# A decoder block at batch 1: another order for the opening, the background loads, the norm and the closing

## The chip, the cores and the metric

The kernel runs on one core of one Trainium2 chip, as a single launch. The metric is the device time of that core in microseconds (us): before the change 1770.57 us, the median of three runs (1770.28 to 1771.84). Smaller is better.

## The reference, cut to what matters

One layer of a decoder block over 256 tokens of width 2048, all in float32:

```python
mod = (silu(c) @ ada_w + ada_b)          # shift_m, scale_m, gate_m, shift_f, scale_f, gate_f
h = rmsnorm(x) * (1 + scale_m) + shift_m
p = h @ w_in                             # gla q,k,v,output gate,decay; mla q and kv latents, rope key; two gates
y_gla = (rmsnorm(gla_chunked(q, k, v, log_a)) * silu(p_g)) @ gla_wo     # 4 heads
y_mla = mla_attention(...) @ mla_wo                                     # 16 heads, rotary part
x = x + gate_m * ((sigmoid(p_ga) * y_gla + sigmoid(p_gb) * y_mla) @ w_out)
h = rmsnorm(x) * (1 + scale_f) + shift_f
x = x + gate_f * ((silu(h @ W_g) * (h @ W_u)) @ ffn_w_down)             # hidden width 5632
return rmsnorm(x)
```

## The kernel before

**Weights.** Each weight is read from DRAM once, in halves of two k-tiles of 128 rows by 512 columns (512 KB, `load_raw`, L100). ScalarE casts a half to a high part (L111), VectorE subtracts to get the low part (L112), and `form_a` (L164) or `form_b` multiplies both with the high and low part of the activations: three products per tile (L170 to L172), 12 matmuls of 512 columns a half in `form_a`. The raw tiles are a ring of six, with more of them where `more_raw` lends other memory; the high and low tiles are rings of three.

**The order.** The program is written engine by engine in one Python order; a planner with a model of the engines then decides, for each engine, which of its ready instructions is issued next, and the engines run that list in order. So an instruction may be issued far ahead of where it is written. `tc.keep_in_program_order(i)` puts `i` behind the instruction written before it on the same engine, without a wait for its end.

**Background work.** The modulation vectors come from `ada_w`, six blocks of 2048 columns. `ada_steps(m, c0)` (L270) is a generator that loads eight halves, one a yield, and leaves two VectorE dots for each (L282, L284); for m of 2, 3 and 4 it then reduces over the partitions on GpSimd (L294) and yields once more. `tick()` (L158) comes after each weight half: it issues the dots left, takes `pace[0]` more yields from the list `bg`, and moves two lanes of attention work on by a step. `background(1000)` (L871) takes all that is left.

**The stages.** The opening (L398 to L425) loads x, broadcasts silu(c) into `crow`, squares and transposes x, takes 1/rms by Newton steps (`rsqrt_mean`, L195), spreads it along the free axis (`rows_of`, L211), and forms the first two k-tiles of shift and scale by dots with `ada_t` (`ada_cols`, L247). `rope_angles` (L348) reduces the rotary angles on GpSimd, `rope_tables` (L382) turns them into sine and cosine. Four passes over `w_in` follow (r = 0 to 3), each with 16 jobs; `rope_tables` is called after the job of index 0 in the last pass. Then eight pairs of MLA heads with seven ticks each (`mla_pair`, L612; `pace` 0.2, L728), beside the GLA attention; the output gate O_G with 32 ticks (L781, 0.6), in whose first head the MLA heads still live are stepped to their end (L783 to L785); `mla_wo` with 32 ticks (0.8); `gla_wo` with 32 (0.65, L822); `w_out` with eight for each of four column groups (0.6, L855). In the last of these, i = 3, `background(1000)` runs first, and the last two halves are kept and multiplied token tile by token tile (L883). Then the norm: x1 is squared with a running sum (L890), 32 transposes fill x1T (L905), and 16 modulations (`modulate`, L318) give the input of the FFN. The FFN's halves follow, then `ffn_w_down`, whose last four k-tiles are held and multiplied at the end, block by block, with the closing behind each block: gate (L1008), add (L1009), square (L1011), for two of four blocks a multiply with the final gain on GpSimd (L1013), and after the fourth the sum, the Newton steps and the scalings (L1014 to L1023).

## Time and profile before

| | |
|---|---|
| median of three runs | 1770.57 us |
| the profiled execution | 1769.9 us |
| its span, first to last instruction | 1768.1 us |
| TensorE busy | 1694.1 us, 96% |
| VectorE busy | 1235.1 us, 70% |
| ScalarE busy | 832.2 us, 47% |
| GpSimd busy | 121.2 us, 7% |
| mean granted TensorE clock | 0.98 |
| DMA | 418.31 MB, mean 237 GB/s |

PE is TensorE, PEld its weight loads, which run beside it; DVE is VectorE, ACT ScalarE, POOL GpSimd, SP the engine that issues most of the DMA. DMA rates count all queues. The span is shorter than the execution by what lies ahead of the first instruction and behind the last. Busy times of different engines overlap, so they don't add up to the span; what counts is where the engine with the most work waits, and what ended that wait.

### The profile page before, as it was taken

What the parts mean: (1) busy time and instruction counts of PE and PEld (TensorE: products, weight loads), DVE (VectorE), ACT (ScalarE), POOL (GpSimd) and SP (SyncE); (2) the same over time, 40 slices, a digit from 0 to 9 for tenths busy, and PEclk for the clock granted to TensorE, in tenths of its full rate; (3) what the DMA queues carried; (4) which work ended last, traced back from release to release, by engine and by line L of the source; (5) the groups of instructions that cost most, each with busy time, mean ns of one, the idle gap of its engine ahead of it and who ended that gap; (6) DMA issues with size and microseconds to landing.
All of it is one profiled execution on the core that took longest, in us unless ns stands there. A gap on an engine that the chain in (4) does not pass through costs nothing.

```text
span 1768.1 us, 23022 instructions
## 1 busy us (share of the span) xinstructions
PE 1694.1 (96%) x8388; PEld 1427.0 (81%) x8388; DVE 1235.1 (70%) x1797; ACT 832.2 (47%) x1154; POOL 121.2 (7%) x139
## 2 busy tenths in 40 slices
PE   4999999999999999999996799999999999999997
PEld 2998899889998887788884588888888888788885
DVE  5999977587786477999887767667664444555556
ACT  4644434356666555444442254444444444444443
POOL 5000000000000111110011100000000000000001
PEclk7999999999999999999998899999999999999999
DMA  8999986655545487999997658788786666555552
GB/s 300 355 349 322 322 249 195 187 190 150 171 117 187 158 297 242 357 367 317 323 345 261 238 155 273 236 251 270 237 248 189 189 191 190 178 190 187 187 186 108
DMA packets 196074, 418.31 MB, mean 237 GB/s; under 512 B 13060, under 2 KB 23636, under 8 KB 195320
## 3 DMA queue, kind: packets, MB, share of 16 engines
q1 hardware_dynamic: 194136, 410.27, 71.0%
q0 software_dynamic: 1680, 6.51, 1.0%
q8 instruction: 66, 1.08, 0.2%
q14 instruction: 48, 0.39, 0.1%
q10 hardware_dynamic: 144, 0.07, 0.0%
HBM read 410.49 MB, written 6.30 MB: 236 GB/s over the span
## 4 chain that ended last, share of the span: by engine, by line
PE 90%; DVE 4%; POOL 2%; issue 2%; DMA 1%; ACT 1%; DVEq 0%; ACTq 0%; POOLq 0%
PE mm L171 20%; PE mm L172 20%; PE mm L170 20%; PE mm L180 3%; PE mm L181 3%; PE mm L182 3%; PE mm L959 2%; PE mm L960 2%; PE mm L961 2%; PE gx L685 2%; PE gx L960 1%; PE aux L960 1%; PE aux L959 1%; PE gx L959 1%; PE aux L961 1%
## 5 line engine op out<-in xcount | busy, mean ns | idle before, releaser
L112 DVE TENSOR_TENSOR lo<-raw,hi 128x1024 fp32r<-128x1024 f32 (+3 forms) x518 | 599.7, 1163 | 356.6 <-ACT hi L111 354.3
L111 ACT CAST hi<-raw 128x1024 fp32r<-128x1024 f32 (+3 forms) x518 | 506.5, 984 | 567.6 <-PE mm L172 400.1
L171 PE MATMUL mm<-lo,s 128*128 128x512 f32 (+1 forms) x1648 | 647.1, 393 | 2.4 <-DVE lo L112 2.2
L172 PE MATMUL mm<-hi,s 128*128 128x512 f32 (+1 forms) x1648 | 640.9, 390 | 0.0
L170 PE MATMUL mm<-hi,s 128*128 128x512 f32 (+1 forms) x1648 | 587.1, 392 | 22.8 <-ACT hi L111 21.6
L170 PEld LDWEIGHTS mm<-hi,s 128*128 128x128 f32 x1648 | 310.3, 189 | 88.7 <-ACT hi L111 24.3
L171 PEld LDWEIGHTS mm<-lo,s 128*128 128x128 f32 x1648 | 311.8, 189 | 67.5 <-DVE lo L112 6.0
L172 PEld LDWEIGHTS mm<-hi,s 128*128 128x128 f32 x1648 | 311.7, 189 | 61.6 <-issue 0.7
L284 DVE SCALAR_TENSOR_TENSOR ada<-raw,cact,ada 128x512 f32<-128x512 f32 x191 | 143.0, 749 | 15.4 <-DMA raw<-in_ada_w_dram 12.8
L111 ACT CAST hi<-s 128x1024 fp32r<-128x1024 f32 (+1 forms) x65 | 67.5, 1039 | 114.5 <-PE mm L172 66.6
L180 PE MATMUL mm<-s,hi 128*128 128x256 f32 x416 | 118.5, 287 | 0.0
L181 PE MATMUL mm<-s,hi 128*128 128x256 f32 x416 | 117.4, 284 | 0.0
L182 PE MATMUL mm<-s,lo 128*128 128x256 f32 x416 | 115.4, 285 | 0.0
L112 DVE TENSOR_TENSOR lo<-s,hi 128x1024 fp32r<-128x1024 f32 (+1 forms) x65 | 80.3, 1236 | 32.0 <-ACT hi L111 31.6
L180 PEld LDWEIGHTS mm<-s,hi 128*128 128x128 f32 x416 | 79.6, 191 | 0.8 <-issue 0.3
L181 PEld LDWEIGHTS mm<-s,hi 128*128 128x128 f32 x416 | 79.6, 191 | 0.4
L182 PEld LDWEIGHTS mm<-s,lo 128*128 128x128 f32 x416 | 78.3, 191 | 0.0
L960 PE MATMUL mm<-lo,w 128*128 128x512 f32 x160 | 63.6, 398 | 0.0
L294 POOL PARTITION_ALL_REDUCE ada<-ada x12 | 45.2, 3763 | 269.5 <-DVE ada L284 269.5
L961 PE MATMUL mm<-hi,w 128*128 128x512 f32 x160 | 62.6, 393 | 0.0
L959 PE MATMUL mm<-hi,w 128*128 128x512 f32 x160 | 50.9, 396 | 0.7 <-ACT w L968 0.7
L968 ACT CAST w<-s 128x256 fp32r<-128x256 f32 x44 | 17.7, 408 | 59.1 <-PE aux L960 59.1
(274 smaller groups left out, 1694.4 us busy)
## 6 DMA issues: line engine op xcount, KB each, us to landing
raw<-in_ffn_w_in_dram SPq DMA_DIRECT2D x176, 512.0 KB, 4.5
raw<-in_w_in_dram SPq DMA_DIRECT2D x124, 512.0 KB, 4.9
raw<-in_ada_w_dram SPq DMA_DIRECT2D x102, 512.0 KB, 4.8
raw<-in_ffn_w_down_dram SPq DMA_DIRECT2D x88, 512.0 KB, 4.4
raw<-in_ada_t_dram SPq DMA_DIRECT2D x44, 512.0 KB, 5.9
s<-in_ada_w_dram SPq DMA_DIRECT2D x26, 512.0 KB, 6.7
s<-in_w_in_dram SPq DMA_DIRECT2D x23, 512.0 KB, 4.4
raw<-in_mla_wo_dram SPq DMA_DIRECT2D x20, 512.0 KB, 5.6
```

The lines of the kernel that those rows point to most:

```text
L111: A.copy(out=hh_, in_=rr)
L112: V.tensor_tensor(out=ll_, in0=rr, in1=hh_.bitcast(F32), op=ALU.subtract)
L170: T.matmul(ps[t][:, :cols], lhsT=ah[:, k, ts], rhs=hi, start=st, stop=False)
L171: T.matmul(ps[t][:, :cols], lhsT=ah[:, k, ts], rhs=lo, start=False, stop=False)
L172: T.matmul(ps[t][:, :cols], lhsT=al[:, k, ts], rhs=hi, start=False, stop=en)
L180: T.matmul(o, lhsT=hi[:, pick], rhs=ah[:, k], start=st, stop=False, skip_group_check=True)
L181: T.matmul(o, lhsT=hi[:, pick], rhs=al[:, k], start=False, stop=False, skip_group_check=True)
L182: T.matmul(o, lhsT=lo[:, pick], rhs=ah[:, k], start=False, stop=en, skip_group_check=True)
L284: ins = V.scalar_tensor_tensor(out=acc, in0=raw[:, k - k0], scalar=c, in1=acc, op0=ALU.mult, op1=ALU.add)
L959: T.matmul(o, lhsT=ah[:, ts], rhs=hi[:, ns], start=first, stop=False)
L960: T.matmul(o, lhsT=ah[:, ts], rhs=lo[:, ns], start=False, stop=False)
L961: T.matmul(o, lhsT=al[:, ts], rhs=hi[:, ns], start=False, stop=last)
```

## The change

No product is added or left out; orders change.

- Opening: the copies of `crow` come first; x and the first eight loads of `ada_t` are issued in one fixed order (x's first half, four loads, x's second half, four loads), the dots in the same order on VectorE, six of them ahead of the Newton steps and two behind; the Newton steps and the scaled identity are pinned one behind the other. `ada_cols` is split into `ada_dots` and `ada_mod`. `rope_angles` is written later, and the instructions of `rope_tables` are pinned where they are written.
- Pace: 0.2 becomes 0.4 in the MLA stage, 0.65 becomes 0.8 in `gla_wo`, 0.6 becomes 0.75 in `w_out`.
- Heads: the stepping of the last MLA heads to their end leaves the first head of O_G; two slots for the GLA output are taken where they are first needed (`og_slots`), which steps the heads to their end if they still live.
- Norm: the transposes from k = 4 on are issued behind the last matmul of `w_out`; the casts of the second and third half split after the norm's modulations are issued behind the last Square.
- Closing: the first token tile's four scalings are one VectorE instruction each, issued behind the second tile's adds; the second tile's two multiplies with the gain move from GpSimd to VectorE.

`follow(a, b)` puts `a` behind `b` on their engine in the same way as the pin. Cut to its core:

```diff
         for rr, hh_, ll_ in ((raw, hv, lv),) if perm is None else perm(raw, hv, lv):
-            A.copy(out=hh_, in_=rr)
+            h = A.copy(out=hh_, in_=rr)
+            if fence:
+                follow(h, fence.pop(0))
             V.tensor_tensor(out=ll_, in0=rr, in1=hh_.bitcast(F32), op=ALU.subtract)
         return [(hv[:, k], lv[:, k]) for k in range(kk)]
+
+    fence = []
+
+    def follow(ins, prev):
+        if prev is not None:
+            tc.add_manual_dep(ins.ins, prev.ins.name, mybir.DependencyInfo(
+                mybir.DependencyClass.NoSync, mybir.DependencyReason.DATA), reason="order on one engine")
...
+        return mm
...
-    def rsqrt_mean(dst, ssq, n, w, eng=None):
+    def rsqrt_mean(dst, ssq, n, w, eng=None, pinned=False):
         v, l = sb(w, "rv"), sb(w, "rl")
+        pin = tc.keep_in_program_order if pinned else lambda i: i
+        pin(V.tensor_scalar(out=v, in0=ssq, scalar1=1.0 / n, scalar2=EPS, op0=ALU.mult, op1=ALU.add))
...
-    def rows_of(col, dst):
+    def rows_of(col, dst, pinned=False):
+        pin = tc.keep_in_program_order if pinned else lambda i: i
...
-    def ada_cols(k, now=False):
+    def ada_dots(k, now=False):
         for m in (1, 0):
...
                 raw = raw_tile()
-                nc.sync.dma_start(out=raw, in_=ada_t[m * D + k * P:m * D + (k + 1) * P, hf * 1024:(hf + 1) * 1024])
+                d = nc.sync.dma_start(out=raw, in_=ada_t[m * D + k * P:m * D + (k + 1) * P, hf * 1024:(hf + 1) * 1024])
...
                 if now:
-                    dot()
+                    tc.keep_in_program_order(d)
+                    tc.keep_in_program_order(dot())
                 else:
...
         flush()
+
+    def ada_mod(k):
         V.scalar_tensor_tensor(out=mod[:, 16 + k:17 + k], in0=mod[:, 16 + k:17 + k], scalar=1.0, in1=nmg[:, k:k + 1],
...
         modulate(k, xTk, rx, 0, hhk, hlk)
+
+    def ada_cols(k):
+        yield from ada_dots(k)
+        ada_mod(k)
...
         four = sb(512, "sc", 2)
-        V.scalar_tensor_tensor(out=ang2, in0=ang, scalar=-1.0, in1=ang, op0=ALU.mult, op1=ALU.max)
+        pin(V.scalar_tensor_tensor(out=ang2, in0=ang, scalar=-1.0, in1=ang, op0=ALU.mult, op1=ALU.max))
         V.tensor_scalar(out=ang2, in0=ang2, scalar1=-1.0, scalar2=float(np.float32(np.pi / 2)), op0=ALU.mult,
...
         for i, a in enumerate((ang, ang2)):
-            A.copy(out=four[:, i * S:(i + 1) * S].rearrange("p (t r f) -> p t r f", t=2, r=4),
-                   in_=a.rearrange("p (t f) -> p t f", t=2).unsqueeze(2).broadcast_to([P, 2, 4, 32]))
-            for t in range(2):
-                c = slice(i * S + t * P, i * S + (t + 1) * P)
-                T.transpose(out=ps[:, c], in_=four[:, c], identity=ident)
-        A.activation(out=sin_t, in_=ps[:, 0:S], func=AF.Sin, scale=sgn)
+            pin(A.copy(out=four[:, i * S:(i + 1) * S].rearrange("p (t r f) -> p t r f", t=2, r=4),
+                       in_=a.rearrange("p (t f) -> p t f", t=2).unsqueeze(2).broadcast_to([P, 2, 4, 32])))
+        for i in range(4):
+            c = slice(i * P, (i + 1) * P)
+            pin(T.transpose(out=ps[:, c], in_=four[:, c], identity=ident))
+        pin(A.activation(out=sin_t, in_=ps[:, 0:S], func=AF.Sin, scale=sgn))
         A.activation(out=cos_t, in_=ps[:, S:2 * S], func=AF.Sin)
...
     sx, rc2 = sb(2, "sx"), sb(2, "rx")
-    for t in range(2):
-        tc.keep_in_program_order(nc.sync.dma_start(out=xtok[:, t], in_=x[0, t * P:(t + 1) * P]))
-    ang, ang2 = rope_angles()
+    pin = tc.keep_in_program_order
     for b in range(4):
...
         T.matmul(ps, lhsT=ones, rhs=d, start=True, stop=True)
-        A.copy(out=crow[:, 512 * b:512 * (b + 1)], in_=ps)
+        pin(A.copy(out=crow[:, 512 * b:512 * (b + 1)], in_=ps))
+    more_raw((qk, 0, 4))
+    first = [ada_dots(k, True) for k in range(2)]
     for t in range(2):
-        A.activation(out=vt[:, 0:2048], in_=xtok[:, t], func=AF.Square, accum_out=sx[:, t:t + 1])
+        pin(nc.sync.dma_start(out=xtok[:, t], in_=x[0, t * P:(t + 1) * P]))
+        pin(A.activation(out=vt[:, 0:2048], in_=xtok[:, t], func=AF.Square, accum_out=sx[:, t:t + 1]))
+        for _ in range(4 - 2 * t):
+            next(first[t])
     for k in range(0, KT, 2):
         x_blocks(k)
-    rsqrt_mean(rc2, sx, D, 2)
-    rows_of(rc2, rx)
-    more_raw((qk, 0, 4))
+    rsqrt_mean(rc2, sx, D, 2, pinned=True)
+    rows_of(rc2, rx, pinned=True)
+    for _ in first[1]:
+        pass
+    for _ in first[0]:
+        pass
+    ang, ang2 = rope_angles()
     for k in range(2):
-        for _ in ada_cols(k, True):
-            pass
+        ada_mod(k)
     lat = slot(4)
...
         bg += [ada_steps(m, 512 * b) for m in (4, 3)]
-    pace[0] = 0.2
+    pace[0] = 0.4
     GLA.wait += [gla_att(h) for h in range(GH)]
...
     gtv = gt.rearrange("p (t d) -> p t d", t=2)
-    ogh, ogl = slot(6, F32R), slot(7, F32R)
-    oghk, oglk = k256(ogh), k256(ogl)
+    og = []
+
+    def og_slots():
+        if not og:
+            while ATT.busy():
+                ATT.step()
+            og[:] = [k256(slot(i, F32R)) for i in (6, 7)]
+        return og
...
         yield
+        oghk, oglk = og_slots()
         for k in range(0, 4, 2):
...
         ps = full(form_a, w_in, O_G + 512 * h, hhk, hlk, KT)
-        if h == 0:
-            while ATT.busy():
-                ATT.step()
+        assert h < 2 or not ATT.busy()
         if h == 0:
...
-    pace[0] = 0.65
+    pace[0] = 0.8
     mh, ml = slot(2, F32R), slot(1, F32R)
...
     for i in range(4):
-        for n, ps in enumerate(group(form_a, gla_wo, 512 * i, oghk, oglk, KT)):
+        for n, ps in enumerate(group(form_a, gla_wo, 512 * i, *og, KT)):
             tick()
...
     sq = sb(8, "sq")
-    pace[0] = 0.6
+    pace[0] = 0.75
...
             for k, w in kept:
-                form_a(ps, w, k256(mh), k256(ml), k, False, k == KT - 2, 512, (t,))
+                last = form_a(ps, w, k256(mh), k256(ml), k, False, k == KT - 2, 512, (t,))
             u = sb(512, "sc", 2)
...
             V.tensor_tensor(out=x1v[:, t, cs], in0=x1v[:, t, cs], in1=u, op=ALU.add)
-            A.activation(out=u, in_=x1v[:, t, cs], func=AF.Square, accum_out=sq[:, j:j + 1])
+            sqr = A.activation(out=u, in_=x1v[:, t, cs], func=AF.Square, accum_out=sq[:, j:j + 1])
             if j in (3, 5):
...
             for t in range(2):
-                T.transpose(out=ps[:, kk * S + t * P:kk * S + (t + 1) * P],
-                            in_=x1v[:, t, (k + kk) * P:(k + kk + 1) * P], identity=ident)
+                tp = T.transpose(out=ps[:, kk * S + t * P:kk * S + (t + 1) * P],
+                                 in_=x1v[:, t, (k + kk) * P:(k + kk + 1) * P], identity=ident)
+                if k >= 4:
+                    follow(tp, last)
         A.copy(out=x1T[:, k * S:(k + 2) * S], in_=ps)
...
         modulate(k, x1k, r2, 3, k256(fh), k256(fl))
+    fence[:] = [None, sqr, sqr]
     more_raw()
...
     otv = ot.rearrange("p (t d) -> p t d", t=2)
+    def finish(t, fr, behind):
+        for n, prev in zip((2, 0, 3, 1), behind):
+            ns = slice(n * 512, (n + 1) * 512)
+            if n < 2 and t:
+                A.activation(out=otv[:, t, ns], in_=x1v[:, t, ns], func=AF.Copy, scale=fr)
+            else:
+                follow(V.scalar_tensor_tensor(out=otv[:, t, ns], in0=x1v[:, t, ns], scalar=fr, in1=fg[:, ns],
+                                              op0=ALU.mult, op1=ALU.mult), prev)
+            nc.sync.dma_start(out=out[0, t * P:(t + 1) * P, ns], in_=otv[:, t, ns])
+
+    frs = []
     for t in range(2):
...
         fr = sb(1, "fr", 2)
+        adds = []
         for n in range(4):
...
             V.tensor_tensor(out=u, in0=acc[t][n], in1=gate_f[:, ns], op=ALU.mult)
-            V.tensor_tensor(out=d, in0=d, in1=u, op=ALU.add)
+            adds.append(V.tensor_tensor(out=d, in0=d, in1=u, op=ALU.add))
             junk = sb(512, "sc", 2)
             A.activation(out=junk, in_=d, func=AF.Square, accum_out=fs[:, n:n + 1])
-            if n < 2:
-                G.tensor_tensor(out=d, in0=d, in1=fg[:, ns], op=ALU.mult)
+            if n < 2 and t:
+                V.tensor_tensor(out=d, in0=d, in1=fg[:, ns], op=ALU.mult)
         V.tensor_reduce(out=f1, in_=fs, axis=AX.X, op=ALU.add)
         rsqrt_mean(fr, f1, D, 1)
-        for n in (2, 0, 3, 1):
-            ns = slice(n * 512, (n + 1) * 512)
-            if n < 2:
-                A.activation(out=otv[:, t, ns], in_=x1v[:, t, ns], func=AF.Copy, scale=fr)
-            else:
-                V.scalar_tensor_tensor(out=otv[:, t, ns], in0=x1v[:, t, ns], scalar=fr, in1=fg[:, ns],
-                                       op0=ALU.mult, op1=ALU.mult)
-            nc.sync.dma_start(out=out[0, t * P:(t + 1) * P, ns], in_=otv[:, t, ns])
+        frs.append(fr)
+    finish(0, frs[0], (adds[1], adds[2], adds[3], adds[3]))
+    finish(1, frs[1], (None,) * 4)
```

## Rows read from the trace of the kernel before

**Rows 1.** The page: engines' busy time; TensorE's slices; issues of one load.

```profile
PE 1694.1 (96%) x8388; PEld 1427.0 (81%) x8388; DVE 1235.1 (70%) x1797; ACT 832.2 (47%) x1154; POOL 121.2 (7%) x139
...
PE   4999999999999999999996799999999999999997
...
raw<-in_ada_w_dram SPq DMA_DIRECT2D x102, 512.0 KB, 4.8
```

**Rows 2.** Waits of TensorE, whole span: total us, times, longest.

```profile
PE mm L170 <- ACT hi L111: 21.6, 5, 16.0
```

**Rows 3.** Table by stretch: length, busy PE PEld DVE ACT POOL, clock, DMA, GB/s.

```profile
48.00:64.00 16.00, 16.00 (x72) 13.25 (x71) 15.59 (x24) 13.03 (x20) 0.00 (x0) 1.00 1.03 396
380.00:580.00 200.00, 199.93 (x1346) 182.81 (x1345) 149.47 (x362) 131.26 (x292) 6.93 (x8) 1.00 0.50 157
774.00:795.50 21.50, 21.50 (x97) 17.80 (x96) 19.10 (x29) 9.15 (x10) 3.23 (x1) 1.00 1.03 373
795.50:885.40 89.90, 89.90 (x410) 74.45 (x409) 80.38 (x110) 40.50 (x43) 7.72 (x2) 1.00 0.92 321
953.40:1006.80 53.40, 30.12 (x104) 21.96 (x104) 37.04 (x65) 12.79 (x17) 8.56 (x4) 0.74 0.69 241
```

**Rows 4.** The same table for the instructions of L284 alone.

```profile
795.50:885.40 89.90, 27.15 (x37) 1.00 0.92 321
953.40:1006.80 53.40, 21.77 (x29) 0.74 0.69 241
```

**Rows 5.** Timeline of the opening: start, us, instruction [idle before <- what ended it].

```profile
12.46 1.28 DVE L256 CUSTOM_DVE_ANT_0 raw<-raw,s,vec 128x1024 f32<-128x1024 f32 x1 [6.74 <-DMA raw<-in_ada_t_dram]
...
25.78 0.37 ACT L219 COPY s<-aux 128x256 f32<-128x256 f32 x1 [5.96 <-PE aux L216]
...
36.90 0.24 POOL L379 TENSOR_SCALAR s<-s 128x64 f32<-128x64 f32 x1
37.17 0.41 ACT L389 COPY sc<-s 128x256 f32<-128x256 f32 x1 [9.50 <-POOL s L379]
...
37.63 0.69 PE L393 MATMUL aux<-ident,sc 128*128 128x128 f32 x2 [11.89 <-ACT sc L389]
...
38.58 1.22 PE L170 MATMUL mm<-hi,s 128*128 128x512 f32 x2 [0.26 <-ACT hi L111]
```

**Rows 6.** Timeline, TensorE at the start of the O_G stage.

```profile
602.96 0.33 PE L592 MATMUL aux<-ident,sc 128*128 128x128 f32 x1 [2.16 <-ACT sc L587]
```

**Rows 7.** Timeline of `w_out`: VectorE, SyncE's queue, ScalarE.

```profile
930.24 1.28 DVE L888 TENSOR_TENSOR sc<-mm,s 128x512 f32<-128x512 f32 x2
...
952.73 1.37 DVE L888 TENSOR_TENSOR sc<-mm,s 128x512 f32<-128x512 f32 x2 [3.98 <-PE mm L172]
...
965.62 1.94 SPq L102 DMA_DIRECT2D s<-in_w_out_dram  x2
...
971.10 1.04 ACT L111 CAST hi<-s 128x1024 fp32r<-128x1024 f32 x1 [14.07 <-DMA s<-in_w_out_dram]
```

**Rows 8.** Timeline around the norm: transposes of an earlier group, then its chain.

```profile
936.43 1.04 PE L905 MATMUL aux<-ident,s 128*128 128x128 f32 x8
...
1006.78 0.69 DVE L888 TENSOR_TENSOR sc<-mm,s 128x512 f32<-128x512 f32 x1
1007.38 1.22 DVE L112 TENSOR_TENSOR lo<-raw,hi 128x1024 fp32r<-128x1024 f32 x1
...
1016.56 1.26 DVE L321 SCALAR_TENSOR_TENSOR e<-s,mod,aux 128x256 f32<-128x256 f32 x3 [1.38 <-PE aux L216]
...
1017.63 0.80 PE L170 MATMUL mm<-hi,s 128*128 128x512 f32 x1 [1.12 <-ACT s L322]
```

**Rows 9.** Timeline of the closing: last matmul, reduction, last scalings.

```profile
1756.27 0.39 PE L961 MATMUL aux<-s,w 128*128 128x512 f32 x1
...
1759.49 0.16 DVE L1014 TENSOR_REDUCE f<-fs 128x1 f32<-128x4 f32 x1 [0.85 <-ACT sc L1011]
...
1761.81 1.42 DVE L1021 SCALAR_TENSOR_TENSOR s<-s,fr,s 128x512 f32<-128x512 f32 x2
```

More of the change, by code (lines that the diff above doesn't have):

```diff
@@ L171, in form_a @@
                 T.matmul(ps[t][:, :cols], lhsT=ah[:, k, ts], rhs=lo, start=False, stop=False)
-                T.matmul(ps[t][:, :cols], lhsT=al[:, k, ts], rhs=hi, start=False, stop=en)
+                mm = T.matmul(ps[t][:, :cols], lhsT=al[:, k, ts], rhs=hi, start=False, stop=en)
+        return mm
     def form_b(ps, w, ah, al, k0, first, last, cols, blocks=None):
@@ L252, in ada_cols @@
                 raw = raw_tile()
-                nc.sync.dma_start(out=raw, in_=ada_t[m * D + k * P:m * D + (k + 1) * P, hf * 1024:(hf + 1) * 1024])
+                d = nc.sync.dma_start(out=raw, in_=ada_t[m * D + k * P:m * D + (k + 1) * P, hf * 1024:(hf + 1) * 1024])
                 def dot(raw=raw, hf=hf, c=c, part=part):
-                    V.tensor_tensor_reduce(out=raw, in0=raw, in1=crow[:, hf * 1024:(hf + 1) * 1024], scale=1.0,
-                                           scalar=part if hf else cb[:, c:c + 1], op0=ALU.mult, op1=ALU.add,
-                                           accum_out=mod[:, c:c + 1] if hf else part)
+                    return V.tensor_tensor_reduce(out=raw, in0=raw, in1=crow[:, hf * 1024:(hf + 1) * 1024], scale=1.0,
+                                                  scalar=part if hf else cb[:, c:c + 1], op0=ALU.mult, op1=ALU.add,
+                                                  accum_out=mod[:, c:c + 1] if hf else part)
                 if now:
-                    dot()
+                    tc.keep_in_program_order(d)
+                    tc.keep_in_program_order(dot())
                 else:
```

14 lines of the change are left out of this document (7 added, 7 removed).

## The prediction

> **What bounds the kernel now.** I read the page first, for each engine's share and the slices: TensorE is busy 1694.1 of 1768.1 us and most slices stand at 9 [rows 1]. So at most 74 us can be won from waiting, plus what runs at the half clock, and the question is only where TensorE waits. The list of waits gives the answer in one line: 21.6 us for the casts of L111, one of them 16.0 [rows 2]. Then the table by stage: in four stretches TensorE is busy throughout, and in 953.4 to 1006.8, the last column group of `w_out`, 30.12 of 53.40, at a mean granted clock of 0.74 [rows 3]. The timeline then shows what ended those waits. The span has four places that are not full: the opening (first weight matmul at 38.58) [rows 5], a gap of 2.16 at 603 [rows 6], the last `w_out` group with the norm behind it [rows 7, 8], and the tail [rows 9]. Everything else is TensorE's own work.
>
> **The pace: what is still to drain.** The 12 `ada_steps` of this stretch give 9 yields each (8 loads, one after the reduction): 108 units. Ticks times pace, before: 56 x 0.2 + 32 x 0.6 + 32 x 0.8 + 32 x 0.65 + 24 x 0.6 = 91.2, so 16.8 units are left when `background(1000)` comes at i = 3. The trace has them: 29 dots of L284 stand in that stretch, 21.77 us of VectorE [rows 4]. Their loads stand on SP's queue ahead of the last `w_out` halves; the queue waits for raw tiles that the dots free one by one, the first `w_out` load is issued at 965.62, and ScalarE's cast starts at 971.10 after 14.07 us of waiting for it [rows 7]. After: 22.4 + 19.2 + 25.6 + 25.6 + 24 x 0.75 = 110.8, more than 108. The list is empty about three ticks before i = 3 and the drain finds nothing.
> The price of the stall: the i = 2 group took 952.73 - 930.24 = 22.49 us, eight transposes of 1.04 in it [rows 7, 8]; the i = 3 group 53.4 [rows 3]. Difference **-30.9**. The half clock is inside this number, as TensorE fell to it after the 16 us of waiting; no wait, no fall.
> What the earlier units cost: 11.2 more units fall into the MLA stage, some 20 dots of 27.15/37 = 0.734 us [rows 4] = 14.6 us of VectorE, which is busy 149.47 of 200 there, and 10 loads of 512 KB [rows 1], where DMA runs at 157 GB/s [rows 3]. TensorE's queue hides it. The four m = 2 steps also write `gm_sp` from SP, pinned there; two of the four now come in the MLA stage, with weight loads queued behind, but 2.5 ticks lie between the reduction and that write, so I count nothing. In the `gla_wo` stage VectorE is the tight place: 80.38 of 89.90 busy [rows 3], and 0.8/0.65 x 37 = 45.5 dots add 8.5 x 0.734 = 6.2, so 86.6, 96%. If that cover is gone TensorE waits for the lower halves of L112. The nearest row with pace 0.8 has VectorE at 19.10 of 21.50 and TensorE full [rows 3]. Bounds 0 to +8; I take **+2**, nearer to that row. DMA: 8 + 5.7 + 1 loads of 0.524 MB in 21.9 us are 352 GB/s; that row shows 373 with TensorE full, so nothing.
>
> **The opening.** `rope_tables` is written after the first job of the last pass, but its order on each engine was left to the planner, which put it ahead of the first weights. GpSimd ends the angles at 36.90 + 0.24; ScalarE, in order, waits 9.50 us on them, the transposes of L393 11.89, and the cast of the first weights stands behind [rows 5]. The change pins these instructions behind the first job of the last pass; then the next thing late is `rx`: its copy at 25.78 takes 0.37 [rows 5], then a modulation and the cast of `hh`, which in the FFN's norm take 1017.63 - 1016.56 = 1.07 from the same broadcast to the first matmul [rows 8], so 27.2. From 38.58 that is -11.4. The reordering of x, dots and Newton steps: eight dots now run from 12.46 on, when the first load after both halves of x is in [rows 5], and the scaled identity comes last; afterwards four dots can run before the second half of x is in, the Newton steps are issued in one piece behind six dots, and two dots and the modulation's scalar are queued behind them. On SP the second x (1 MB) now stands behind four loads of 0.5 MB, so the Square starts later, by up to 2.1 MB at the 396 GB/s of [rows 3], 5.3 us. Bounds -3 to +3; I take -1, since what ends the new chain is the eighth dot, which starts earlier. Against it: at 38.58 DMA had filled every buffer; starting 12 us earlier, the first pass needs 16 + 16.8 loads of 0.524 MB in 16 x 12 matmuls x 0.225 us = 43.2 us, 398 GB/s, and 48 to 64 shows 396 with TensorE full and VectorE at 15.59 of 16 [rows 3]. That is just enough: 0 to +5, I take +1. Sum **-11.4**.
> The Trainium skill (DMA: Bandwidth & Descriptors, section "Where 436 GB/s comes from") says that the HBM side binds a load at about 358 GB/s per core. By that, an estimate, the 17.2 MB would take 48 us and the opening would give 4.8 less; the 396 GB/s of the trace speak against it.
> The four transposes and two copies now fall into a full stage, and the first of them waits on VectorE, which has its adds queued behind: 0.5 to 2, I take **+0.7**.
>
> **The norm.** 24 of 32 transposes (k from 4 on) now follow the last matmul of the projection. 16 of them leave two full groups: two times 1.04, pipelined 0.9 each, **-1.8**; they return in the wait for the norm. That wait is 1017.63 - 1006.78 = 10.85 us [rows 8]. At its start VectorE runs two lower halves (1.22; the first of the two is shown) and the L888 and L889 of the first token tile (0.69 each, overlapped about 1.2) between the last matmul and the Square. With the drain gone, the first tile's pair falls under the last six matmuls and, with the casts of the second and third FFN half held behind the last Square, the two lower halves go too: 1.2 + 2.4 = 3.6. They may come back between the Newton steps, which are not pinned here. Bounds -3.6 to -1.2; I take one coming back, **-2.4**. Behind the held casts on ScalarE stand only later casts; TensorE needs them 2.7 us after its first FFN matmul.
>
> **The last heads.** The drain stands after eight ticks of `O_G`, and two heads need two more steps each; as I read the code it drains nothing, and only the allocation of two slots moves. The gap of 2.16 [rows 6] comes from ScalarE's chain of softmax steps. Bounds -4 to +2, I take 0.
>
> **The closing.** The GpSimd multiplies leave and four VectorE scalings come instead of two and two on ScalarE for the first tile, two of them (0.71 each [rows 9]) behind the last add. TensorE ends at 1756.66, the reduction of the last sum starts at 1759.49, 2.83 later [rows 9]. New: L1008 and L1009 of the last block at the 0.69 of L888 [rows 8] are 1.4, two scalings 1.4, so 2.8 as before, where L1008 was late. The last Square lies beside the scalings. Bounds -0.6 to +1.4, I take **0**.
>
> **Sum.** -30.9 + 2 - 11.4 + 0.7 - 1.8 - 2.4 + 0 + 0 = -43.8. The span falls from 1768.1 to 1724.3, the profiled execution from 1769.9 to 1726.1; the median of the runs shown lies 0.7 above that execution, so **1726.8**.
>
> **Rivals.** (A) VectorE becomes the bound in the `gla_wo` and `w_out` stages: at 96% any misplaced dot makes TensorE wait; for it the 96%, against it the full TensorE at pace 0.8. The full 8 us: 1733. (B) The first pass is bound by its supply, since it starts without the stock of loads: for it the 398 GB/s wanted, against it the 396 shown; 5 instead of 1, so 1731. By the 358 GB/s of the Trainium skill (DMA: Bandwidth & Descriptors, same section), an estimate, it would be this case. (C) The other side: in the MLA stage the ring has six raw tiles shared by weights and ada loads; if each of the 11.2 more units makes TensorE wait for a load that lands after 4.8 us [rows 1], 54 us are lost and the time is 1781. It decides from 43.8/11.2 = 3.9 us a unit. Against it: pace 0.6 with the same ring, right after 603, loses only the one gap. (D) The change doesn't do what it says: a wait of the rope tables or a remainder of units stays in TensorE's way. If only the opening works (-11.4 + 0.7): 1760; if only pace and norm: 1738.
>
> **How the numbers follow.** Forecast 0.60, its own range 1719 to 1734 (the bounds of opening, norm and heads); A 0.17, B 0.12, C 0.03, D 0.08. Range 1717 to 1742: all favourable bounds together would give about 1716, and the top takes in A with B and the milder half of D. 0.2% is 3.5 us, about what a measurement of this kernel tells from no change. Faster by more: all but C and a rest for unseen waits, 0.95; within: 0.02; slower: 0.03.
>
> **What would show it.** Right: first L170 at 25 to 29 us, no L393 before it; no L284 after the third `w_out` group, that group's successor in about 22 us at full clock; 24 transposes right behind the last matmul and 7 to 10 us from there to the FFN; GpSimd idle at the end. Wrong: TensorE waiting on L112 between 780 and 920, on L111 in the first pass or the MLA stage, or an L170 that waits for raw loads at i = 3.

## The result, and the profile after

The changed kernel takes 1749.47 us, median of four runs (1748.79 to 1749.99), beside 1770.68 before (four runs): ratio 0.9879, 95% interval [0.9862, 0.9896], some 21 us faster. The forecast was 1726.8 with a range of 1717 to 1742, so half of the forecast gain came. The page of the kernel after, to be read beside [rows 1], shows how busy each engine is:

```profile
PE 1696.2 (97%) x8388; PEld 1428.7 (82%) x8388; DVE 1230.2 (70%) x1801; ACT 829.6 (47%) x1152; POOL 124.7 (7%) x135
...
PE   6999999999999999799999899999999999999997
```

The opening's slice has gone from 4 to 6, and of the hole at `w_out` (67) the norm's slice is left, an 8. But at the 17th place, 699 to 743 us, stands a 7 that was a 9. The list of TensorE's waits (total us, times, longest) says on what, to be read beside [rows 2]:

```profile
PE mm L180 <- DVE lo L114: 9.5, 7, 6.4
...
PE mm L179 <- ACT hi L111: 5.9, 2, 5.3
...
PE gx L802 <- DVE s L792: 2.5, 2, 2.2
PE mm L190 <- ACT s L647: 2.1, 1, 2.1
```

The 21.6 us on the casts are 5.9 now, nearly all in the opening. New are a wait of 6.4 on the lower half of a weight (L114 is L112 of before), one of 2.2 on a gated head's scaling (L792), one of 2.1 on the copy of an MLA query (L647).

Marks in both traces (start of the last instruction named) tell where the difference arises:

| mark | before | after | difference |
|---|---|---|---|
| first weight matmul | 38.58 | 30.11 | -8.5 |
| last copies of the first pass (out of TensorE's `mm` banks) | 91.6 | 84.7 | -6.9 |
| last key copies of the MLA stage | 591.0 | 589.5 | -1.5 |
| low part of the MLA output, first piece (end of the O_G stage) | 704.2 | 700.2 | -4.0 |
| last gating of `mla_wo` | 796.5 | 805.3 | +8.8 |
| last gating of `w_out` | 1008.5 | 987.1 | -21.4 |
| end of the span | 1768.1 | 1748.2 | -19.9 |

Between the fourth and the fifth mark, 12.8 us are lost that no step of the forecast has. Here is the start of `mla_wo` in the kernel after, GpSimd, then VectorE, then TensorE (start, us, instruction, idle before it and what ended it):

```profile
709.02 0.62 POOL L213 TENSOR_TENSOR rl<-gr 128x2 f32<-128x2 f32 x1 [22.43 <-DVE gr L209]
709.71 0.20 POOL L214 TENSOR_TENSOR rl<-rl,rv 128x2 f32<-128x2 f32 x1
710.00 0.19 POOL L215 TENSOR_SCALAR rl<-rl 128x2 f32<-128x2 f32 x1
719.91 3.25 POOL L314 PARTITION_ALL_REDUCE ada<-ada  x1 [9.72 <-issue]
730.03 0.19 POOL L216 TENSOR_TENSOR gr<-gr,rl 128x2 f32<-128x2 f32 x1 [6.87 <-issue]
...
708.83 0.75 DVE L304 SCALAR_TENSOR_TENSOR ada<-raw,cact,ada 128x512 f32<-128x512 f32 x1
...
714.91 1.23 DVE L114 TENSOR_TENSOR lo<-s,hi 128x1024 fp32r<-128x1024 f32 x1 [1.48 <-ACT hi L111]
723.19 0.29 DVE L321 CUSTOM_DVE_ANT_0 ada<-ada,ident 128x128 f32<-128x128 f32 x1 [7.06 <-POOL ada L314]
...
724.45 1.22 DVE L114 TENSOR_TENSOR lo<-raw,hi 128x1024 fp32r<-128x1024 f32 x1
...
725.72 0.79 PE L180 MATMUL mm<-lo,s 128*128 128x512 f32 x1 [6.43 <-DVE lo L114]
733.28 0.33 PE L802 MATMUL gx<-ident,s 128*128 128x128 f32 x1 [2.21 <-DVE s L792]
```

Read it from the top. The last gated head takes its 1/rms by 12 Newton steps on GpSimd. The planner has put a background all-reduce after the third of them. The all-reduce's input is ready at 709.58 (L304), GpSimd's last step ends at 710.19, yet the all-reduce starts at 719.91, and GpSimd waits for nothing that the profile shows ("issue"). After it, 6.87 us pass until the fourth Newton step. So here, where the next instruction's input is ready, a change of kind on GpSimd costs 9.72 us one way and 6.87 the other. It has two victims. VectorE's queue holds the four dots that read the all-reduce (L321) ahead of a weight's lower half (L114); VectorE stands for 7.06 us, TensorE for 6.43, and then runs at the half clock (0.50 granted in 724 to 728). And the head itself is late, for which TensorE waits at 733.28. In 700 to 760 TensorE loses 9.70 us of idle time and 3.5 by the clock (the shortfall of the granted clock times the busy time, summed over windows of 4 us). The same stretch before lost 1.30 and nothing by the clock. The rows of the table by stretch (columns as in [rows 3]), before and after:

```profile
690.00:760.00 70.00, 68.70 (x302) 54.92 (x301) 64.34 (x89) 33.60 (x41) 13.27 (x20) 1.00 0.92 330
```

```profile
690.00:760.00 70.00, 60.30 (x246) 47.10 (x245) 50.60 (x76) 28.97 (x37) 8.79 (x14) 0.93 0.80 273
```

The second new place is the passage from the last pass to the MLA stage. The same table of the kernel after:

```profile
384.00:392.00 8.00, 5.43 (x31) 4.19 (x30) 7.09 (x12) 2.36 (x5) 0.53 (x1) 1.00 0.71 227
392.00:396.00 4.00, 3.94 (x21) 3.94 (x22) 3.99 (x9) 1.67 (x4) 0.53 (x1) 0.61 0.47 177
```

And its timeline there, VectorE, then ScalarE:

```profile
382.86 0.75 DVE L304 SCALAR_TENSOR_TENSOR ada<-raw,cact,ada 128x512 f32<-128x512 f32 x1 [0.95 <-DMA raw<-in_ada_w_dram]
...
384.47 0.74 DVE L304 SCALAR_TENSOR_TENSOR ada<-raw,cact,ada 128x512 f32<-128x512 f32 x1
...
385.46 0.68 DVE L499 TENSOR_TENSOR s<-mm,s 128x512 f32<-128x512 f32 x1
...
391.42 0.59 ACT L647 COPY s<-mm 128x512 f32<-128x512 f32 x1 [1.83 <-DMA ga_sp<-s]
```

TensorE loses 2.6 us idle and 1.5 at a mean clock of 0.61. The last pass's additions (L499) stand behind background additions (L304), one of which waits for its load; so the write of that tile to DRAM (`ga_sp`) is late, and with it the copy of the first MLA query into the same memory, whose bank TensorE wants.

### The profile page after: what moved, and what is told of

It is laid out like the page before. It is cut to its first block, busy times and chain, and to the rows that moved or that the text cites. A ratio compares the mean times of both kernels' runs of the same rounds, so it can differ in the third digit from the quotient of the medians.

```text
span 1748.2 us, 23021 instructions
## 1 busy us (share of the span) xinstructions
PE 1696.2 (97%) x8388; PEld 1428.7 (82%) x8388; DVE 1230.2 (70%) x1801; ACT 829.6 (47%) x1152; POOL 124.7 (7%) x135
## 4 chain that ended last, share of the span: by engine, by line
PE 87%; DVE 5%; DMA 3%; issue 3%; ACT 2%; POOL 0%; SPq 0%; DVEq 0%; ACTq 0%; POOLq 0%
PE mm L180 19%; PE mm L181 19%; PE mm L179 19%; PE mm L190 3%; PE mm L192 3%; PE mm L191 3%; PE mm L994 2%; PE mm L993 2%; PE mm L995 2%; DVE lo L114 2%; PE gx L711 1%; PE gx L994 1%; PE aux L994 1%; PE aux L993 1%; PE gx L993 1%
## 5 line engine op out<-in xcount | busy, mean ns | idle before, releaser
L114 DVE TENSOR_TENSOR lo<-raw,hi 128x1024 fp32r<-128x1024 f32 (+3 forms) x520 | 597.7, 1156 | 348.1 <-ACT hi L111 343.8
L180 PE MATMUL mm<-lo,s 128*128 128x512 f32 (+1 forms) x1648 | 648.0, 393 | 9.6 <-DVE lo L114 9.5
L180 PEld LDWEIGHTS mm<-lo,s 128*128 128x128 f32 x1648 | 311.5, 189 | 76.5 <-DVE lo L114 14.9
L304 DVE SCALAR_TENSOR_TENSOR ada<-raw,cact,ada 128x512 f32<-128x512 f32 x195 | 145.9, 748 | 15.3 <-DMA raw<-in_ada_w_dram 12.8
L114 DVE TENSOR_TENSOR lo<-s,hi 128x1024 fp32r<-128x1024 f32 (+1 forms) x63 | 77.5, 1230 | 31.6 <-ACT hi L111 31.4
L314 POOL PARTITION_ALL_REDUCE ada<-ada x12 | 46.8, 3899 | 261.2 <-DVE ada L304 251.5
```

What stands on the lines that cost most here:

```text
L114: V.tensor_tensor(out=ll_, in0=rr, in1=hh_.bitcast(F32), op=ALU.subtract)
L180: T.matmul(ps[t][:, :cols], lhsT=ah[:, k, ts], rhs=lo, start=False, stop=False)
L304: ins = V.scalar_tensor_tensor(out=acc, in0=raw[:, k - k0], scalar=c, in1=acc, op0=ALU.mult, op1=ALU.add)
```

## The experiments

Each is timed in three rounds beside the kernel before, in the same session; differences are taken between ratios to it, at 1770 us. The 95% interval of a ratio is some 2.6 us to either side, so times alone don't tell a difference of under about 4 us between two of these kernels from none; where a smaller one is named, it rests on the trace.

### Is it the split chain, and whose is it?

The new paces alone on the kernel before:

```diff
-    pace[0] = 0.2      # MLA
+    pace[0] = 0.4
-    pace[0] = 0.65     # gla_wo
+    pace[0] = 0.8
-    pace[0] = 0.6      # w_out
+    pace[0] = 0.75
```

> The kernel before with the new paces alone (0.4 in the MLA stage, 0.8 in gla_wo, 0.75 in w_out). Theory 1 (the split chain: the new pace moves an all-reduce of GpSimd into the middle of the last head's Newton steps, and VectorE's queue stands behind it): w_out -31 as the raw loads of the fourth group are gone, +12 at the start of mla_wo, +2.7 in gla_wo: about -16, 1754 to 1756, and the trace shows the all-reduce near 720 with under 12 Newton steps ahead of it and TensorE waiting about 6 us on a VectorE split. Rival 2 (the mla_wo stall comes from the heads that are no longer drained alone, or from the shifted opening): no such stall here, about -29, 1740 to 1743.

1757.28, ratio 0.9926 [0.9911, 0.9941]: -13. Here are GpSimd and TensorE (L294 is L314 of after, L171 its L180):

```profile
727.32 3.25 POOL L294 PARTITION_ALL_REDUCE ada<-ada  x1 [10.30 <-issue]
737.24 0.18 POOL L205 TENSOR_TENSOR gr<-gr,rl 128x2 f32<-128x2 f32 x1 [6.67 <-issue]
...
733.13 0.80 PE L171 MATMUL mm<-lo,s 128*128 128x512 f32 x1 [7.68 <-DVE lo L112]
```

The same stall without opening, heads, norm or closing: it is the pace's. So is the loss at the MLA stage: 2.6 us on L621 (L647 of after) stand in this trace too. The counterpart is the changed kernel with the three old paces:

> The changed kernel with the old paces (0.2, 0.65, 0.6). Theory 1: the stall at the start of mla_wo goes and the 31 us in w_out come back: 1749.5 - 12 - 2.7 + 31 = about 1766; opening, heads and norm alone are left, and if the 4 us lost between the last pass and the MLA stage (us 386 to 394) are the opening's or the rope tables' they are still in the trace. Rival 2: the stall stays, 1778 or more. Rival 3 (the 4 us between the passes and the MLA stage come from the new pace): they are gone, about 1762.

1763.83, ratio 0.9965 [0.9952, 0.9977]. No wait in 690 to 760 is over 0.7 us, 384 to 400 is full, and in `w_out` TensorE waits 23.1 us on casts again. Rival 3 of this run holds for the passage: the new pace makes it. The two parts, -13 and -6, add up to the whole change within the scatter.

Next, the Newton steps of the gated heads on VectorE:

```diff
-        rsqrt_mean(r, st, GDV, 2, G)
+        rsqrt_mean(r, st, GDV, 2)
```

> The changed kernel with the Newton steps of the four gated heads on VectorE (9 small instructions a head) in place of GpSimd (12), so that GpSimd runs nothing but all-reduces after the opening. Theory 1: no all-reduce is behind another kind of GpSimd work, the waits of 6.4, 2.2 and 0.3 us at 725 to 734 go with their half clock: -10 to -13, 1737 to 1739. Rival 2 (VectorE is what is full there, GpSimd only the last to be seen): 36 small VectorE instructions more make it worse, 1749 to 1753.

1737.15, ratio 0.9814 [0.98, 0.9829]: -11.5 against the changed kernel. VectorE and GpSimd in this kernel:

```profile
708.07 0.75 DVE L304 SCALAR_TENSOR_TENSOR ada<-raw,cact,ada 128x512 f32<-128x512 f32 x1
...
708.98 3.23 POOL L314 PARTITION_ALL_REDUCE ada<-ada  x1 [44.35 <-DVE ada L304]
```

The stretch from 690 to 760, where the changed kernel has TensorE busy for 60.30 and VectorE for 50.60 of 70:

```profile
690.00:760.00 70.00, 68.83 (x303) 54.83 (x302) 62.51 (x107) 32.54 (x40) 7.43 (x2) 1.00 0.93 328
```

With no other work on GpSimd the all-reduce starts 0.16 us after its input, where it took 10.3 in the kernel after. VectorE does more and waits less: it was not full, it was held. What GpSimd does in those gaps the profile names only as a configuration instruction of some 10 ns in its queue; counted for the all-reduce's line they are, in the changed kernel and in this one,

```profile
L314 POOLq MODIFY_POOL_CONFIG  x10: 7/11/12, 395.4 to 732.7; - x10
```

```profile
L314 POOLq MODIFY_POOL_CONFIG  x2: 7/10/12, 395.0 to 395.1; - x2
```

ten and two (name, count, least, median and longest ns, first and last start). They come in pairs, so that is five set-ups and one: with one kind of work left, GpSimd is set up for it once.

Last, the chain stays on GpSimd, but an all-reduce recorded after a chain goes behind it:

```diff
+                tail[:] = [eng.tensor_tensor(out=dst, in0=dst, in1=l, op=ALU.mult)]
...
+            if tail:
+                follow(red, tail.pop())
```

> The changed kernel with one order edge: an all-reduce of the background goes behind the whole Newton chain that was recorded before it, not into it. The chain stays on GpSimd. Theory 1 in its full form (two victims: the chain itself, and VectorE's queue behind the all-reduce): the chain's wait (2.2 + 0.3 us at 733) goes, the all-reduce still starts only about 7 us after the last Newton step (gaps of 6.7 to 8 us stand ahead of each all-reduce that follows other GpSimd work), near 720, so the 6.4 us of VectorE's queue stay unless the dots that read it move back: -2 to -4, 1745 to 1748. Rival 2 (only the split itself costs, the order change is enough): -10 to -13, 1737 to 1739.

1744.2, ratio 0.9851 [0.9836, 0.9866]: -5. GpSimd, then TensorE:

```profile
722.61 3.25 POOL L314 PARTITION_ALL_REDUCE ada<-ada  x1 [7.88 <-issue]
...
728.41 0.80 PE L180 MATMUL mm<-lo,s 128*128 128x512 f32 x1 [5.04 <-DVE lo L114]
```

The chain's wait is gone, VectorE's is still 5 us: the two victims part as the full form of theory 1 says. So it is not the split alone that costs: the all-reduce still starts 7.88 us after the chain, with its input long there, and VectorE's order is written for one that starts at once.

### One background unit later

`pace[1]` is the remainder that the ticks add up; starting from -1 the first unit of the MLA stage comes at its fifth tick instead of its third or earlier:

```diff
-    pace[0] = 0.4
+    pace[:] = [0.4, -1.0]
```

> The changed kernel with the first background unit of the MLA stage at its fifth step, as in the kernel before, and from there at the new pace. Theory (the 2.1 + 0.4 us of waits and the half clock at 386 to 396 are VectorE's queue: the last pass's additions stand behind an ada addition that waits for its load, so the spill of their tile and the copy into it are late): that stall goes, -3.5 to -4.5. All units then come a step or two later, and if that takes the all-reduce out of the Newton chain at 710 too, another -10 to -12: 1745 to 1746 or 1733 to 1736. Rival (the spill's transfer itself is what is slow): the stall stays.

1732.8, ratio 0.9778 [0.9764, 0.9793]: -18 against the changed kernel, -39 against before. GpSimd in this kernel, then VectorE's last background addition ahead of it:

```profile
716.36 4.11 POOL L314 PARTITION_ALL_REDUCE ada<-ada  x1 [7.95 <-DVE ada L304]
...
715.48 0.74 DVE L304 SCALAR_TENSOR_TENSOR ada<-s,cact,ada 128x512 f32<-128x512 f32 x1
```

And its two stretches:

```profile
384.00:392.00 8.00, 8.00 (x60) 7.57 (x59) 7.32 (x15) 4.34 (x8) 0.00 (x0) 1.00 0.55 178
...
690.00:760.00 70.00, 68.69 (x295) 53.79 (x294) 61.46 (x94) 33.59 (x40) 10.87 (x14) 1.00 0.93 328
```

Both stalls are gone. All 24 Newton steps of the last two heads stand ahead of this all-reduce, and the last ends at 708.41. The input of the all-reduce is complete only at 716.22 (715.48 + 0.74), and it starts 0.14 us later. So this all-reduce is not late at all: the change of kind lies in time in which GpSimd waits for the input anyway, and its dots come at 721.25, after its end at 720.47. The changed kernel has such a place too: the all-reduce at 620.32 starts 7.37 us behind a chain and 0.13 behind its input. The stall is a matter of phase: it needs an input that is ready soon after the other kind of work, and weights behind its reader, and the planner's order decides whether one all-reduce meets both. The same late unit with the paces alone, on the kernel before:

> The kernel before with the new paces and the late first unit alone: opening, heads, norm and closing as before. Theory (the pace's own worth is what was forecast, -30.9 + 2 = -29, and only the split chain and the 4 us at the MLA stage hid half of it): 1770.6 - 29 = 1741 to 1743, no wait of 5 us or more on a VectorE split near 715 to 735. Rival (the raw loads that leave w_out cost more in the stages that take them): 1748 or more.

1739.33, ratio 0.9825 [0.9808, 0.9841]: -31, where -29 was forecast for the pace. And with the VectorE steps as well:

> The changed kernel with both: the Newton steps of the gated heads on VectorE and the first background unit of the MLA stage late. Theory (two separate losses of the new pace, about 12 us from the split Newton chain and about 4 us between the last pass and the MLA stage; each of the two edits takes the chain's split away, only the late unit also the 4 us): 1737.2 - 4 = 1733, no gain over the late unit alone (1732.8), which had both already. Rival (the two edits act on different parts of one stall): 1720 to 1728.

1735.55, ratio 0.9804 [0.9789, 0.9819]. The gains don't add, as the theory says. By the ratios it is 4.6 us more than with the late unit alone; the trace has new waits of 1.1 and 0.5 us on the first `mla_wo` halves, the first of which is cast at 710.2 instead of 707.2, and of 2.2 and 0.5 us at 747.

### The norm

```diff
-    fence[:] = [None, sqr, sqr]
+    fence[:] = [None, cp, cp]     # cp: the last copy into x1T
```

> The changed kernel with the second and third cast of the FFN's first weights ordered behind the last copy of the transposed x1 instead of behind the last square. Theory (the norm gained nothing because these two casts free two VectorE splits of 1.22 us each that then stand inside the Newton steps, 991.1 to 993.5): 10.84 us from the last w_out matmul to the first FFN matmul become 7.5 to 9, so -2 to -3.3, 1746.2 to 1747.5, and no split is left between the Newton steps. Rival (the weights are needed at once: the casts come late and the first FFN group waits for them): the wait moves to the FFN's first splits, 1749 to 1751.

1749.73, ratio 0.9876 [0.9859, 0.9892]: no difference that can be measured. In the trace the stretch from the first transpose behind the last `w_out` matmul to the first FFN matmul takes 9.6 us instead of 10.8: the two lower halves have left the Newton steps, but stand ahead of the first modulated block. So the chain was pinned down to the row, with the casts behind the second modulated block, on top of the kernel with late unit and VectorE steps:

```diff
-    rsqrt_mean(rc2, sq[:, 6:8], D, 2)
+    rsqrt_mean(rc2, sq[:, 6:8], D, 2, pinned=True)
...
-    fence[:] = [None, sqr, sqr]
+    fence[:] = [None, first_md, first_md]
```

> The kernel of the last entry (Newton steps on VectorE, late unit) with the norm's row pinned on VectorE from its first step to the row, and the FFN's second and third cast ordered behind the second modulated block. Theory (10.8 us from the last w_out matmul to the first FFN matmul hold 2.4 us of weight splits, which moved from the Newton steps to ahead of the first modulated block when only the casts were moved): 7.3 to 8.7 us there, and 2 to 3 us less than the last entry, 1730 to 1731, unless the FFN's second pair of blocks then waits for its casts (rival: same time, the wait a few matmuls later).

1731.75, ratio 0.9789 [0.9773, 0.9805]; the wait is 8.2 us, 2.6 less. (The total is 2.7 less, which by itself would be within the scatter.) Without the VectorE steps:

> The changed kernel with the late first unit and the norm's casts and row as in the entry with 8.2 us there, the Newton steps of the gated heads back on GpSimd. Theory (both gains add; the VectorE Newton steps cost the entries that had them some 2 us of new waits at the start of mla_wo): 1732.8 - 2.6 = 1730, the fastest so far. Rival: 1731.8 to 1733, no gain over either.

1730.14 (1729.13 to 1731.89), ratio 0.9774 [0.9757, 0.979]: the lowest time here, 40 us below before and 18 to 19 below the changed one. By the ratios this is only 0.7 us below the kernel with the late unit alone (0.9778), so the norm's gain is shown by the wait, 8.35 us against 10.85 there, and not by the total. TensorE around the norm, with VectorE's lower halves now behind the first modulations:

```profile
968.84 1.04 PE L937 MATMUL aux<-ident,s 128*128 128x128 f32 x8
...
975.30 0.77 PE L229 MATMUL aux<-e,ones 128*128 128x256 f32 x2 [1.84 <-DVE e L227]
977.19 0.80 PE L179 MATMUL mm<-hi,s 128*128 128x512 f32 x1 [1.11 <-ACT s L342]
...
976.11 1.26 DVE L341 SCALAR_TENSOR_TENSOR e<-s,mod,aux 128x256 f32<-128x256 f32 x3 [0.96 <-PE aux L229]
...
978.87 2.35 DVE L114 TENSOR_TENSOR lo<-raw,hi 128x1024 fp32r<-128x1024 f32 x2
```

### The heads

The last heads drained at the first gated group again (`og_slots()` called at h == 0), on the changed kernel and on the one with late unit and VectorE steps:

> The changed kernel with the last heads drained alone again at the first gated group. Theory (the heads' idle time of 2.2 us and the half clock behind it were worth 3 us in the changed kernel): +2 to +3.5, 1751.5 to 1753. Rival, as forecast (0, since the work only moves): 1749 to 1750. A shift of the plan that takes the all-reduce out of the Newton chain would show as -10 or more and would speak for the split chain as a matter of phase.

> The first kernel of this call with the last heads drained alone again, as in the kernel before. Forecast's step (0: the same head work either way, -4 to +2): 1732 to 1734. Rival (a drain without filler costs the 2.2 us of idle time and 1.6 us of half clock that stood behind it in the kernel before): 1735 to 1737.

1749.99, ratio 0.9882 [0.9867, 0.9898], and 1736.38, ratio 0.9809 [0.9794, 0.9823]: the same as without, twice. The gap of [rows 6] is 0.35 in the changed kernel and 2.16 again in both kernels with the late unit, drained or not, so the drain has no part in it. The new pace has: the gap is 0.35 with the paces alone on the kernel before, and 2.16 with the old paces on the changed one.

### The opening

The ring of load tiles turned, so that the first `w_in` load takes a free tile:

```diff
     background(2)
+    turn[0] += RAW - 2
```

> The changed kernel with the ring of load tiles turned so that the first three loads of the first pass go to tiles that are free from the start, not to ones that VectorE's dot products still read. Theory (the opening is bound by the landing of the first w_in tile at 29.0, whose load could go out only at 18.56, and not by the norm's row at 24.8): the load goes out before 12, the first weight matmul starts at 26.5 to 27.5 instead of 30.1: -2.5 to -3.5, 1746 to 1747. Rival (the loads share one supply of some 400 GB/s, so the later ones are late by as much): first matmul earlier but TensorE waits in the first pass, 1748.5 to 1750.

1751.33, ratio 0.9886 [0.9872, 0.9901]: the rival. The load goes out at 11.49, the first weight matmul starts at 28.06, but TensorE waits 1.62 us for a cast at 44.59 and the first pass's last copies (85.3) are no earlier. Three runs on the kernel with the late unit then asked what gives it back: the first with the 16 background loads cut to a sixteenth, the second with their dots cut to a sixteenth, the third with the small loads and the turned ring. All three leave part of the modulation vectors out of the result.

> The changed kernel with the late first unit; the 16 background loads of the first pass (modulation vectors of blocks 2 to 5) bring 64 of their 1024 columns, and the dot products run over these repeated to 960, so that this part of the result is left out but VectorE's work stays. Theory S (the opening gave 4.5 us less than forecast because the loads share a supply of about 400 GB/s): the first w_in tile lands by 25, first weight matmul at 26.5 to 28 instead of 30.1, the last copies of the first pass at 80 to 82 instead of 84.1, total 1729 to 1731. Theory V (VectorE, busy 3.9 of 4 us there, sets the first pass): first matmul at 29.5 to 30.5, 1732 to 1734. Theory R (the ring: the load cannot go out before 18.56): first matmul moves by under 1 us, the rest of the pass not at all.

> The changed kernel with the late first unit; the same 16 loads come whole, and their dot products read 64 of 1024 columns (that part of the result is left out). Theory S: nothing moves by more than 1 us except where a load waits for a dot to free its tile: 1732 to 1734. Theory V: last copies of the first pass at 80 to 82, 1729 to 1731.

> The kernel with the 16 small loads, and the first loads of w_in in tiles that are free from the start. Theory S: what the early load alone gave back in the pass (first matmul at 28.1, but last copies at 84.3) stays won here: first matmul at 26.5 to 28, last copies at 79 to 81.5, 1728 to 1730. Theory V: last copies at 83 to 85 again.

1743.05 (ratio 0.9845 [0.983, 0.986]), 1731.35 (0.9779 [0.9765, 0.9794]) and 1752.72 (0.9902 [0.9887, 0.9917]). The first pass, 30 to 62 us, in the changed kernel, with less traffic, and with less VectorE work:

```profile
30.00:62.00 32.00, 31.33 (x135) 25.68 (x136) 30.84 (x43) 22.92 (x35) 20.58 (x23) 0.88 1.02 383
```

```profile
30.00:62.00 32.00, 28.36 (x124) 22.83 (x124) 31.93 (x51) 20.22 (x30) 22.44 (x23) 0.90 0.71 211
```

```profile
30.00:62.00 32.00, 31.83 (x150) 26.59 (x151) 21.03 (x46) 24.23 (x37) 12.16 (x20) 0.93 1.04 396
```

With less traffic the first matmul does start earlier, at 27.92, but DMA falls to 211 GB/s and TensorE waits more: VectorE is busy 31.93 of 32, with 14 dots and 11 lower halves in this stretch where the kernel with the late unit has 12 and 12, so the planner, given loads that land sooner, put dots ahead of lower halves. The pass ends at 85.9 (84.1 with the late unit) and, with the turned ring, at 93.5; the rest of what these two kernels lose comes later, with further waits for lower halves of 1.3 to 2.5 us between 155 and 200. So these two runs do not measure what bandwidth is worth. With a sixteenth of the dots the pass ends 1.3 us earlier (82.8 instead of 84.1) and the total does not move by more than the scatter. What remains: VectorE and the loads are both nearly full in this pass, and relieving VectorE by itself gives 1.3 us; what relieving the loads would give, these runs don't tell. So rival B, a pass bound by its supply, is neither shown nor excluded, and what an opening relieved of both would give was not tried.

## Why the prediction was wrong, step by step

**The pace: the mechanism right, a side effect missed.** The group i = 3 now stands in this row of the table by stretch of the kernel after:

```profile
963.60:986.70 23.10, 23.10 (x103) 19.10 (x102) 13.68 (x16) 8.72 (x11) 1.27 (x2) 1.00 0.61 213
```

TensorE is full at clock 1.00, where [rows 3] have 30.12 of 53.40 at 0.74. From the last gating of `mla_wo` to that of `w_out` the kernel gained 30.2 us; forecast were -30.9, +2 and -1.8 for pace, `gla_wo` and transposes, together -30.7. (Counted to the last `w_out` matmul, 1006.75 and 986.90, it is 28.7: a lower half of VectorE that stood ahead of the last gating now stands behind it.) The pace alone, with the late unit, measured -31. The step that failed is in "What the earlier units cost": it priced the added units by VectorE's time and DMA's share in the stages that take them, and let TensorE's queue hide the rest ("TensorE's queue hides it"). It put at nothing where each unit's all-reduce would fall on GpSimd and who stands behind its reader in VectorE's queue, and which of VectorE's older work a unit's additions would stand ahead of. The first is 12 us at `mla_wo`, the second 4 us at the passage to the MLA stage. The rivals looked elsewhere too: A at VectorE's load in `gla_wo`, where TensorE waits 1.6 us in all, and C at the ring in the MLA stage. The trace of before gives little warning: the shortest gap between Newton steps and an all-reduce in its 600 to 800 us is 6.78 us, but the profile puts it down to the all-reduce's input, which came 0.8 us before its start:

```profile
725.32 3.46 POOL L294 PARTITION_ALL_REDUCE ada<-ada  x1 [6.78 <-DVE ada L284]
```

No dot reads this one: it belongs to the last `ada_steps` of m = 2, whose sum SyncE writes to `gm_sp` at 729.34, and the first dots on an all-reduce (L301) stand at 758.24, 40 us behind the last Newton chain. At the new pace the fourth of these writes goes out at 664.75, so the first all-reduce with dots of VectorE behind it, of m = 4, meets the Newton steps of the last head. The forecast looked at these writes alone ("so I count nothing") and not at the dots that the next steps have in their place.

The Trainium skill (GPSIMD Engine Reference, section "Instruction dispatch") says that the first call to a freshly loaded GpSimd kernel pays about 6 us, 5.95 measured there, which no instruction of the profile shows, and advises to budget for it. The traces agree in kind and show more: 6.67 to 10.30 us stand as "issue" before an all-reduce or behind it, on the way back too, and none of it is to be seen where the input comes later than that.

**The opening: -6.9 instead of -11.4.** The rope tables left the front as forecast, and the row `rx` is copied at 24.80. But the step took `rx` for the next thing late. Next late was the first `w_in` tile:

```profile
18.56 0.38 SPq L102 DMA_DIRECT2D raw<-in_w_in_dram  x1
...
29.01 1.04 ACT L111 CAST hi<-raw 128x1024 fp32r<-128x1024 f32 x1 [2.36 <-DMA raw<-in_w_in_dram]
...
30.11 1.22 PE L179 MATMUL mm<-hi,s 128*128 128x512 f32 x2 [5.35 <-ACT hi L111]
```

(SyncE's queue, ScalarE and TensorE of the kernel after.) SyncE can issue it only at 18.56, behind dots that free the ring's tiles, and it lands 10.4 us later, where the median of these loads is 4.9: from 16 to 32 us all loads together run at 396 to 409 GB/s, the rate that [rows 3] show for a full stage. That is 2.9 us; another 1.8 us go to the half clock, on which TensorE stays longer here (3.6 us lost instead of 1.8). The early load shows that the 2.9 are not to be had alone: with it TensorE starts at 28.06, 2.1 earlier, bound by the row's modulation as forecast, and the pass ends no earlier. As to the 358 GB/s of the Trainium skill (DMA: Bandwidth & Descriptors, section "Where 436 GB/s comes from"), the loads ran at 396 over the 32 us of the run with fewer dots, so that figure does not bound this kernel on its one core.

**The norm: -1.8 not measured by itself, -2.4 not there.** The 24 transposes stand behind the last matmul as forecast; what their leaving gave is inside the 30.2 above. From the last matmul to the FFN it takes 10.84 us (986.74 to 997.58), as before ([rows 8]: 10.85). The forecast let one of two lower halves come back between the Newton steps; both did (991.13 and 992.35, 1.22 each), and the held casts made the transposes wait 2.33 us for a copy. Held behind the row, in two later kernels, the casts leave a wait of 8.2 and 8.35 us, 2.5 to 2.6 less.

**Heads and closing: 0, right.** The heads' edit gave nothing, twice. That the place itself is some 2 us better in the changed kernel (third to fourth mark) comes with the new pace and was not forecast; it is luck of the planner's order. In the closing the last matmul ends at 1736.62 and the reduction starts at 1739.32, 2.70 later, where 2.8 were forecast; from there to the end of the span 8.9 us pass, 8.6 before [rows 9].

**The sum.** Forecast -43.8, measured about -21. The kernel with the late unit, which has the change and neither stall, is at -39; the 5 us that are left to the forecast are of the size of the opening's 4.5 and the norm's 2.4 less what came better. The forecast's +0.7 for the rope tables came: between 222 and 264 us, where their four transposes now stand (251.68 to 257.72), the lead over the kernel before (start of the same matmul in both) falls from 7.0 to 6.2 us, with TensorE busy throughout. Of its signs, the first weight matmul (30.11 instead of 25 to 29) and the way to the FFN (10.84 instead of 7 to 10) failed; the last `w_out` group without background dots, the transposes and the idle GpSimd at the end came. Faster by over 0.2% was right at 0.95. The range ended at 1742: its upper end added the priced risks and had no room for an order that the planner makes anew.

## What to carry to other kernels

When a change moves background work under a planner, look up every instruction that each unit issues, on each engine, and what stands behind its reader in an in-order queue; busy shares do not show this. On GpSimd, look for an all-reduce whose input is ready within some 10 us of other work on that engine: give the engine one kind only, let the input come later, or write the order for an all-reduce that starts late. If an edit's gain falls short, shift its phase by one unit before redesigning: one number in one line brought 18 of 23 us back.

## What was not expected of the hardware

A change of kind on GpSimd (elementwise to all-reduce and back) took 6.7 to 10.3 us with nothing to wait for in the profile; without a change of kind the all-reduce started 0.16 us after its input. The change runs while GpSimd waits for that input: where it came 7.2 to 7.9 us after the last elementwise step (twice in the changed kernel, once in the one with the late unit), the all-reduce started 0.13 to 0.14 us behind it. Why the same change takes 6.7 us in one place and 10.3 in another, no run here shows.
